# The depthwise convolution of the sample tokens: products with all 31 taps and sums along the taps, in place of 31 small multiply-adds per block

## The chip, the core and the metric

The kernel runs on one core of one Trainium2 chip, in one launch. The metric is the device time of a launch in microseconds (us). A core has five engines with a queue of instructions each, which run beside each other and wait for each other by semaphores: TensorE (PE: matmuls, and PEld for its weight loads), VectorE (DVE), ScalarE (ACT), GpSimd (POOL) and SyncE (SP, here the queue for DMA transfers). Within a queue the order is fixed when the program is built. Matmuls write to PSUM, eight banks of 512 fp32 values per partition; weights and activations lie in SBUF.

## The reference

One step of a two-layer decoder trunk with width 1024, for 272 prompt tokens (16 of them meta tokens) and 8 running sequences of 8 new tokens each. A layer is an FFN half step, a mixer, and a second FFN half step. The mixer projects the normed input to many parts; one branch is gated linear attention, the other a causal depthwise convolution of 31 taps over time, whose inputs for a running sequence start with 30 cached rows:

```python
u = a * jax.nn.sigmoid(ga)
up = jnp.concatenate([conv_buf.astype(u.dtype), u], axis=1)
c = lax.conv_general_dilated(up, w_dw[:, None, :].astype(up.dtype), window_strides=(1,), padding='VALID',
                             dimension_numbers=('NWC', 'WIO', 'NWC'), feature_group_count=CONV_CH) + b_dw
c = jax.nn.silu(rmsnorm(c, conv_norm))
o_conv = c @ w_pw
merged = jax.nn.sigmoid(m_a) * o_gla + jax.nn.sigmoid(m_b) * o_conv
```

All inputs and outputs are fp32.

## The kernel before

Activations lie transposed: 128 channels on the partitions, tokens along the free dimension, eight such blocks (KB) for the 1024 channels. There are 336 tokens in order of prompt, samples and meta (320 in the last layer's later parts). Weights stream from HBM in pieces of up to 128x1024 (`raw`). For fp32 accuracy each piece is split into two parts in a fast matmul format: ACT copies `raw` to `wh` (L214), and VectorE or GpSimd computes `wl = raw - wh` (L215). In the mixer it is GpSimd's work, in the FFNs VectorE's. Each product of a weight block with 336 tokens is three matmuls, eight blocks deep: 24 matmuls.

The mixer of a layer runs in this order: three GLU blocks (`pga`, `pa`), the value projection (`pv`), five more GLU blocks, the query and key projections (`pq`, `pk`), and 24 gate blocks (`pgate`). Into this sequence of products all else is woven. A call of `tick` after every third matmul (L252) takes the next entry of a list of small tasks (the decay chain of the attention, with VectorE's `la`, GpSimd's `lal` and the matmuls `pb`; later the attention heads with `sc`, `probs`, `upd`, `sp`, `pso`, `os`, `upds`, `s`, `o`, `ot`), and then calls `fill` (L231).

`fill` hands out the convolution, as filling for VectorE's queue. It keeps two clocks by a cost table, one of TensorE's work and one of VectorE's (`Clocked`, L98), and as long as VectorE's is less than 1000 ns ahead it takes the next tap from the generator `conv_gen` (L415). A tap is two instructions: a multiply-add of 272 prompt columns (256 in the last layer) into the PSUM bank `acc`, and one of the 64 sample columns into the bank `acs`. Both read `u` (from SBUF) shifted by the tap and the tap's weight, one value per partition, from `vec`, and add to what the tap before left in the bank. The first tap (`TENSOR_SCALAR`) also adds the bias. After tap 31 ACT copies the two banks back over `u` and squares them for the norm (L432 to L436). A task of the last head (`conv_flush`, L752) issues the taps that are left.

PSUM banks come from pools: four for the products (tag `mm`), so that a fifth product has to wait until the first one's bank has been read; two for the small products (`aux`: `upds`, `pso`, `upd`, `nrm`, `pb`); one each for `acc` and `acs` (tags `cv` and `cs`), which the FFNs use as well.

Of the kernel before, what the change touches and what calls it, by code (L numbers as in the profile page):

```python
# [9 lines left out]
F32 = mybir.dt.float32  # L10
F32R = mybir.dt.float32r
U32 = mybir.dt.uint32
AF = mybir.ActivationFunctionType
ALU = mybir.AluOpType

D = 1024
KB = D // 128
DEPTH = 2
META = 16
SEQ = 256  # L20
NS = 8
LS = 8
NSAMP = NS * LS
T = SEQ + NSAMP + META
TY = SEQ + NSAMP
TP = 384
PROMPT = META + SEQ
# [6 lines left out]
TAPS = 31  # L34
# [16 lines left out]
V_F1, V_MIX, V_GLA, V_CN, V_F2, V_BDW = 0, 16, 32, 48, 64, 80  # L51
V_FIN = 96
V_DW = 104
# [44 lines left out]
class Clocked:  # L98
# [4 lines left out]
    def __getattr__(self, name):  # L103
        fn = getattr(self.eng, name)

        def call(*args, **kw):
            out = kw["out"] if "out" in kw else args[0]
            n = 1
            for x in out.shape[1:]:
                n *= x  # L110
            self.add(n * {"reciprocal": 6.25}.get(name, 1.04) + 110.0)
            return fn(*args, **kw)  # L112

        return call
# [3 lines left out]
def trunk_kernel(ctx, tc, wts, x_in, vecs, consts, cumw, masks, wdecay, cache, state,  # L118
                 y_out, sp_out, ss_out, u_out):
    nc = tc.nc  # L120
    PE, ACT, POOL, SP = nc.tensor, nc.scalar, nc.gpsimd, nc.sync
# [5 lines left out]
    DVE = Clocked(nc.vector, dve_time)  # L127
# [10 lines left out]
    tmp = ctx.enter_context(tc.tile_pool(name="tmp", bufs=2))  # L138
# [5 lines left out]
    u = cst.tile([128, KB, UW], F32, name="u")  # L144
    vec = cst.tile([128, NV], F32, name="vec")
# [13 lines left out]
    def vcol(base, l, b, n=KB):  # L159
        return vec[:, base + l * n + b:base + l * n + b + 1]  # L160

    def bank(name, tag="mm", bufs=4):
        return psum.tile([128, 512], F32, tag=tag, name=name, bufs=bufs)
# [202 lines left out]
    def u_sample(b):  # L366
        return u[:, b, UP:UW].rearrange("p (s w) -> p s w", s=NS)

    def mixer(l, norm, next_block):
        last = l == DEPTH - 1  # L370
        n = TY if last else T
        skip = META if last else 0
# [42 lines left out]
        def conv_gen():  # L415
            for b in range(KB):
                while b >= ready[0]:
                    yield 1
                acc = bank("acc", "cv", 1)
                acs = bank("acs", "cs", 1)  # L420
                us = u_sample(b)
                accs = acs[:, 0:NSAMP].rearrange("p (s w) -> p s w", s=NS)
                for i in range(TAPS):
                    wcol = vec[:, V_DW + (l * KB + b) * TAPS + i:V_DW + (l * KB + b) * TAPS + i + 1]
                    for o, src in ((acc[:, skip:PROMPT], u[:, b, skip + i:PROMPT + i]), (accs, us[:, :, i:i + LS])):
                        if i == 0:
                            DVE.tensor_scalar(out=o, in0=src, scalar1=wcol, scalar2=vcol(V_BDW, l, b),
                                              op0=ALU.mult, op1=ALU.add)
                        else:
                            DVE.scalar_tensor_tensor(out=o, in0=src, scalar=wcol, in1=o, op0=ALU.mult, op1=ALU.add)  # L430
                    if i == TAPS - 1:
                        ACT.copy(u[:, b, 0:SEQ], acc[:, META:PROMPT])  # L432
                        ACT.copy(u[:, b, SEQ:TY], acs[:, 0:NSAMP])
                        if not last:
                            ACT.copy(u[:, b, TY:T], acc[:, 0:META])
                        cnorm.add(u[:, b, 0:n], n)  # L436
                    yield 1

        conv = conv_gen()

        def decay_lr():
# [138 lines left out]
        for hd in range(HEADS):  # L580
# [3 lines left out]
                                     op0=ALU.mult, op1=ALU.mult)  # L584
# [240 lines left out]
        w0, w1 = W.use("pw"), W.use("pw")  # L825
# [14 lines left out]
        w0, w1 = W.use("out"), W.use("out")  # L840
# [9 lines left out]
    with tc.manual_schedule():  # L850
# [37 lines left out]
        for l in range(DEPTH):  # L888
            n = TY if l == DEPTH - 1 else T
# [14 lines left out]
        for b in range(KB):  # L904
            DVE.scalar_tensor_tensor(out=h[:, b, 0:TY], in0=h[:, b, 0:TY], scalar=vec[:, V_FIN + b:V_FIN + b + 1],
                                     in1=r[:, 0:TY], op0=ALU.mult, op1=ALU.mult)
# [126 lines left out]
```

## Time and profile before

| | us |
|---|---|
| median of 3 runs | 1631.82 (1631.72 to 1634.56) |
| the profiled execution | 1628.32 |
| its span, from the first instruction to the last | 1626.5 |
| TensorE busy in the span | 1597.0 (98%) |
| VectorE busy in the span | 1079.6 (66%) |
| ACT busy, GpSimd busy | 736.0 (45%), 401.9 (25%) |

The durations below are of the one profiled execution. An instruction's row gives its start and its duration. Instructions of VectorE overlap a little: the next one may start before the end that is shown for the one before it, so what an instruction costs its queue is the time from its start to the next start. Matmuls are pipelined in the same way: those of 336 columns start 0.15 us apart and are shown as 0.32 us long. A row with x2 at its end stands for two instructions in a row and gives the time of both together.

### The profile page before, as it was taken

What the parts mean: (1) busy time and instruction counts of PE and PEld (TensorE: products, weight loads), DVE (VectorE), ACT (ScalarE), POOL (GpSimd) and SP (SyncE); (2) the same over time, 40 slices, a digit from 0 to 9 for tenths busy, and PEclk for the clock granted to TensorE, in tenths of its full rate; (3) what the DMA queues carried; (4) which work ended last, traced back from release to release, by engine and by line L of the source; (5) the groups of instructions that cost most, each with busy time, mean ns of one, the idle gap of its engine ahead of it and who ended that gap; (6) DMA issues with size and microseconds to landing.
All of it is one profiled execution on the core that took longest, in us unless ns stands there. A gap on an engine that the chain in (4) does not pass through costs nothing.

```text
span 1626.5 us, 26968 instructions
## 1 busy us (share of the span) xinstructions
PE 1597.0 (98%) x10516; PEld 1570.4 (97%) x10516; DVE 1079.6 (66%) x2170; ACT 736.0 (45%) x1153; POOL 401.9 (25%) x290
## 2 busy tenths in 40 slices
PE   8999999999999999999999999999999999999997
PEld 7999999999889999999999999999999799999997
DVE  6666445999986666664456564459999766666633
ACT  5433334673546444333343333346645464443432
POOL 0000006576663300000000000066766632000000
PEclk9999999999999999999999999999999999999999
DMA  5554444555544544444446444445555445444352
GB/s 197 189 185 137 136 147 135 163 164 164 157 162 130 165 134 156 142 132 140 145 144 208 150 132 143 153 129 156 174 179 169 156 139 164 148 156 148 120 169 77
DMA packets 77023, 247.78 MB, mean 152 GB/s; under 512 B 8672, under 2 KB 11360, under 8 KB 76640
## 3 DMA queue, kind: packets, MB, share of 16 engines
q1 hardware_dynamic: 76032, 240.16, 46.3%
q10 hardware_dynamic: 864, 5.92, 0.9%
q8 instruction: 82, 1.34, 0.3%
q14 instruction: 45, 0.37, 0.1%
HBM read 230.33 MB, written 15.71 MB: 151 GB/s over the span
## 4 chain that ended last, share of the span: by engine, by line
PE 88%; DVE 6%; DMA 2%; POOL 1%; ACT 1%; issue 1%; SPq 0%; DVEq 0%; POOLq 0%; ACTq 0%
PE pu L134 20%; PE pg L134 20%; PE pd L134 20%; PE pgate L134 9%; PE po L134 4%; PE pw L134 3%; DVE acc L112 2%; PE pa L134 2%; PE pv L134 2%; PE pga L134 2%; PE pk L134 2%; PE pq L134 2%; POOL wl L215 1%; DVE acs L112 1%; PE upds L134 1%
## 5 line engine op out<-in xcount | busy, mean ns | idle before, releaser
L112 DVE TENSOR_TENSOR wl<-raw,wh 128x1024 fp32r<-128x1024 f32 (+3 forms) x331 | 361.7, 1109 | 246.0 <-ACT wh L214 245.4
L214 ACT CAST wh<-raw 128x1024 fp32r<-128x1024 f32 (+4 forms) x457 | 427.3, 954 | 61.1 <-issue 24.9
L215 POOL TENSOR_TENSOR wl<-raw,wh 128x1024 fp32r<-128x1024 f32 (+2 forms) x126 | 283.6, 2270 | 145.2 <-ACT wh L214 135.3
L296 POOL TENSOR_TENSOR ssum<-ssum,sq 128x336 f32<-128x336 f32 (+1 forms) x63 | 56.8, 901 | 1021.9 <-ACT sq L295 1021.7
L112 DVE SCALAR_TENSOR_TENSOR acc<-u,vec,acc 128x272 f32<-128x272 f32 (+1 forms) x480 | 235.1, 490 | 0.0
L134 PE MATMUL pg<-xh,wh 128*128 128x336 f32 (+1 forms) x704 | 223.2, 317 | 6.0 <-ACT wh L214 6.0
L134 PE MATMUL pu<-xh,wh 128*128 128x336 f32 (+1 forms) x704 | 222.1, 315 | 1.4 <-ACT wh L214 1.4
L134 PE MATMUL pu<-xh,wl 128*128 128x336 f32 (+1 forms) x704 | 222.1, 315 | 0.3 <-DVE wl L112 0.3
L134 PE MATMUL pg<-xh,wl 128*128 128x336 f32 (+1 forms) x704 | 222.1, 315 | 0.0
L134 PE MATMUL pg<-xl,wh 128*128 128x336 f32 (+1 forms) x704 | 221.9, 315 | 0.0
L134 PE MATMUL pu<-xl,wh 128*128 128x336 f32 (+1 forms) x704 | 221.9, 315 | 0.0
L134 PE MATMUL pd<-act_hi,wh 128*128 128x336 f32 (+1 forms) x704 | 221.0, 314 | 0.0
L134 PE MATMUL pd<-act_hi,wl 128*128 128x336 f32 (+1 forms) x704 | 220.4, 313 | 0.0
L134 PE MATMUL pd<-act_lo,wh 128*128 128x336 f32 (+1 forms) x704 | 220.2, 313 | 0.0
L134 PEld LDWEIGHTS pg<-xh,wh 128*128 128x128 f32 x704 | 133.0, 189 | 6.4 <-ACT wh L214 6.0
L352 ACT CAST act_hi<-pu 128x336 fp32r<-128x336 f32 (+1 forms) x88 | 38.4, 436 | 218.1 <-DVE pu L112 218.1
L112 DVE SCALAR_TENSOR_TENSOR acs<-u,vec,acs 128x64 f32<-128x64 f32 x480 | 135.3, 282 | 0.0
L134 PEld LDWEIGHTS pu<-xh,wh 128*128 128x128 f32 x704 | 132.9, 189 | 1.8 <-ACT wh L214 1.8
L134 PEld LDWEIGHTS pu<-xh,wl 128*128 128x128 f32 x704 | 132.9, 189 | 0.8 <-DVE wl L112 0.8
L134 PEld LDWEIGHTS pg<-xl,wh 128*128 128x128 f32 x704 | 133.0, 189 | 0.4
L134 PEld LDWEIGHTS pg<-xh,wl 128*128 128x128 f32 x704 | 132.9, 189 | 0.2 <-DVE wl L112 0.2
L134 PEld LDWEIGHTS pu<-xl,wh 128*128 128x128 f32 x704 | 132.9, 189 | 0.0
(209 smaller groups left out, 3229.7 us busy)
## 6 DMA issues: line engine op xcount, KB each, us to landing
raw<-in_wts SPq DMA_DIRECT2D x303, 512.0 KB, 3.6
raw<-in_wts SPq DMA_DIRECT2D x64, 384.0 KB, 3.6
raw<-in_wts SPq DMA_DIRECT2D x64, 320.0 KB, 3.0
s<-in_state SPq DMA_DIRECT2D x16, 512.0 KB, 5.5
out_ss<-s SPq DMA_DIRECT2D x16, 512.0 KB, 5.1
raw<-in_wts SPq DMA_DIRECT2D x16, 344.0 KB, 3.3
u<-in_cache ACTq DMA_DIRECT2D x2, 2424.0 KB, 11.6
out_u<-u SPq DMA_DIRECT2D x16, 303.0 KB, 4.6
```

Source lines behind the costliest of these rows:

```text
L112: return fn(*args, **kw)
L134: PE.matmul(out, a, b, start=start, stop=stop)
L214: ACT.copy(wh[:, cs], raw[:, cs])
L215: eng.tensor_tensor(out=wl[:, cs], in0=raw[:, cs], in1=wh[:, cs].bitcast(F32), op=ALU.subtract)
L296: eng.tensor_tensor(out=self.sum[:, 0:n], in0=self.sum[:, 0:n], in1=sq[:, 0:n], op=ALU.add)
L352: ACT.copy(ah[:, j, 0:n], pu[:, 0:n])
```

## The change

The prompt columns keep their 31 multiply-adds. The sample columns no longer have any. In their place, at four points of a block, two sequences are done at once: one product of `u`'s windows (2 sequences x 8 outputs x 31 taps, read as an overlapping view) with the 31 weights of the block, repeated by a stride of zero, into a PSUM bank (496 of its 512 columns), and two taps of the prompt later one sum along the innermost 31 into 2 x 8 columns of an SBUF tile, `acs`. The bias is added by ACT, whose copy back to `u` becomes an activation with a bias. The planner's clock counts a sum by its input.

```diff
--- before.py
+++ after.py
@@ -108,6 +108,8 @@
             n = 1
             for x in out.shape[1:]:
                 n *= x
+            if name == "tensor_reduce":
+                n *= kw["in_"].shape[-1]
             self.add(n * {"reciprocal": 6.25}.get(name, 1.04) + 110.0)
             return fn(*args, **kw)
 
@@ -417,20 +419,31 @@
                 while b >= ready[0]:
                     yield 1
                 acc = bank("acc", "cv", 1)
-                acs = bank("acs", "cs", 1)
-                us = u_sample(b)
-                accs = acs[:, 0:NSAMP].rearrange("p (s w) -> p s w", s=NS)
+                acs = tmp.tile([128, NS, LS], F32, tag="acs", name="acs", bufs=2)
+                taps = vec[:, V_DW + (l * KB + b) * TAPS:V_DW + (l * KB + b + 1) * TAPS]
                 for i in range(TAPS):
                     wcol = vec[:, V_DW + (l * KB + b) * TAPS + i:V_DW + (l * KB + b) * TAPS + i + 1]
-                    for o, src in ((acc[:, skip:PROMPT], u[:, b, skip + i:PROMPT + i]), (accs, us[:, :, i:i + LS])):
-                        if i == 0:
-                            DVE.tensor_scalar(out=o, in0=src, scalar1=wcol, scalar2=vcol(V_BDW, l, b),
-                                              op0=ALU.mult, op1=ALU.add)
+                    o, src = acc[:, skip:PROMPT], u[:, b, skip + i:PROMPT + i]
+                    if i == 0:
+                        DVE.tensor_scalar(out=o, in0=src, scalar1=wcol, scalar2=vcol(V_BDW, l, b),
+                                          op0=ALU.mult, op1=ALU.add)
+                    else:
+                        DVE.scalar_tensor_tensor(out=o, in0=src, scalar=wcol, in1=o, op0=ALU.mult, op1=ALU.add)
+                    part, step = divmod(i - 3, 6)
+                    if 0 <= part < 4 and step in (0, 2):
+                        ss = slice(2 * part, 2 * part + 2)
+                        if step == 0:
+                            prod = bank("prod", "cs", 1)[:, 0:2 * LS * TAPS].rearrange("p (s w i) -> p s w i", s=2, w=LS)
+                            w0 = u_sample(b)[:, ss, 0:LS]
+                            win = bass.AP(tensor=w0.tensor, offset=w0.offset, ap=list(w0.ap) + [[1, TAPS]])
+                            DVE.tensor_tensor(out=prod, in0=win, op=ALU.mult,
+                                              in1=taps.unsqueeze(1).unsqueeze(1).to_broadcast([128, 2, LS, TAPS]))
                         else:
-                            DVE.scalar_tensor_tensor(out=o, in0=src, scalar=wcol, in1=o, op0=ALU.mult, op1=ALU.add)
+                            DVE.tensor_reduce(out=acs[:, ss], in_=prod, op=ALU.add, axis=mybir.AxisListType.X)
                     if i == TAPS - 1:
                         ACT.copy(u[:, b, 0:SEQ], acc[:, META:PROMPT])
-                        ACT.copy(u[:, b, SEQ:TY], acs[:, 0:NSAMP])
+                        ACT.activation(u[:, b, SEQ:TY], acs.rearrange("p s w -> p (s w)"), AF.Identity,
+                                       bias=vcol(V_BDW, l, b))
                         if not last:
                             ACT.copy(u[:, b, TY:T], acc[:, 0:META])
                         cnorm.add(u[:, b, 0:n], n)
```

Two places of VectorE's queue, as the programs are built (a row per instruction; xN where equal ones follow each other; in brackets the semaphores that it waits on, of which DVE_49 is VectorE's own).

The start of the first channel block of the first layer, before: `u` is the last of the GLU block's writes, then the taps follow in pairs.

```order
L112 TENSOR_TENSOR u<-pa,gate 128x8x8
L112 TENSOR_SCALAR acc<-u,vec 128x272 [waits DVE_49]
L112 TENSOR_SCALAR acs<-u,vec 128x64
L112 SCALAR_TENSOR_TENSOR acc<-u,vec,acc 128x272 [waits DVE_49]
L112 SCALAR_TENSOR_TENSOR acs<-u,vec,acs 128x64 [waits DVE_49]
```

The same place now:

```order
L114 TENSOR_TENSOR u<-pa,gate 128x8x8
L114 TENSOR_SCALAR acc<-u,vec 128x272 [waits DVE_49]
L114 SCALAR_TENSOR_TENSOR acc<-u,vec,acc 128x272 [waits DVE_49] x3
L114 TENSOR_TENSOR prod<-u,vec 128x496
L114 SCALAR_TENSOR_TENSOR acc<-u,vec,acc 128x272 [waits DVE_49] x2
L114 TENSOR_REDUCE acs<-prod 128x16
L114 SCALAR_TENSOR_TENSOR acc<-u,vec,acc 128x272 [waits DVE_49]
L114 TENSOR_TENSOR pga<-pga,rstd 128x336 [waits PE_49]
```

The `acs` between two `acc` are gone; three of four `acc` now stand directly behind another, and each still waits on VectorE's semaphore.

The decay chain of the first layer, between two GLU blocks, before: `la` are its three instructions on VectorE, and 88 taps stand ahead of the first of them.

```order
L112 SCALAR_TENSOR_TENSOR acs<-u,vec,acs 128x64 [waits DVE_49]
L112 SCALAR_TENSOR_TENSOR la<-pz,la 128x512 [waits DMAHW5_49,Activation_49]
L112 TENSOR_TENSOR pa<-pa,rstd 128x336 [waits PE_49]
L112 TENSOR_TENSOR u<-pa,gate 128x16 [waits DVE_49,Activation_49]
L112 TENSOR_TENSOR u<-pa,gate 128x256
L112 SCALAR_TENSOR_TENSOR la<-pz,la 128x512 [waits Pool_49]
```

And now, with 89 taps, 12 products and 12 sums ahead of it:

```order
L114 TENSOR_REDUCE acs<-prod 128x16
L114 SCALAR_TENSOR_TENSOR acc<-u,vec,acc 128x272 [waits DVE_49] x3
L114 SCALAR_TENSOR_TENSOR la<-pz,la 128x512 [waits DMAHW5_49,Activation_49]
L114 TENSOR_TENSOR pa<-pa,rstd 128x336 [waits PE_49]
L114 TENSOR_TENSOR u<-pa,gate 128x16 [waits DVE_49,Activation_49]
L114 TENSOR_TENSOR u<-pa,gate 128x256
L114 SCALAR_TENSOR_TENSOR la<-pz,la 128x512 [waits Pool_49]
```

The instructions that don't belong to the convolution are the same and in the same order; only the number of taps ahead of each has moved by a few. On TensorE, GpSimd and SyncE nothing has moved.

## Rows read from the trace of the kernel before

**Rows 1.** The page: busy us (share) instructions; VectorE's busy tenths in 40 slices.
```profile
PE 1597.0 (98%) x10516; PEld 1570.4 (97%) x10516; DVE 1079.6 (66%) x2170; ACT 736.0 (45%) x1153; POOL 401.9 (25%) x290
...
DVE  6666445999986666664456564459999766666633
```
**Rows 2.** Stretches: length; busy us of PE, PEld, DVE, ACT, POOL; clock, DMA.
```profile
20.00:262.00 242.00, 242.00 (x1582) 242.00 (x1581) 131.75 (x179) 97.03 (x146) 15.25 (x18) 1.00 0.49 158
...
268.00:486.00 218.00, 212.57 (x1404) 203.12 (x1403) 205.18 (x614) 113.22 (x200) 142.01 (x91) 0.98 0.52 161
1080.00:1290.00 210.00, 205.99 (x1398) 196.30 (x1397) 200.50 (x616) 111.36 (x191) 140.42 (x91) 1.00 0.53 167
```
**Rows 3.** Timeline of VectorE among the taps: start us, us, engine, line, operation.
```profile
296.40 0.50 DVE L112 SCALAR_TENSOR_TENSOR acc<-u,vec,acc 128x272 f32<-128x272 f32 x1
296.81 0.28 DVE L112 SCALAR_TENSOR_TENSOR acs<-u,vec,acs 128x64 f32<-128x64 f32 x1
297.00 0.50 DVE L112 SCALAR_TENSOR_TENSOR acc<-u,vec,acc 128x272 f32<-128x272 f32 x1
```
**Rows 4.** Timeline of VectorE at a query block.
```profile
362.81 0.51 DVE L112 SCALAR_TENSOR_TENSOR pq<-pq,rstd 128x336 f32<-128x336 f32 x1
363.36 0.51 DVE L112 TENSOR_TENSOR qt<-pq,qt 128x336 f32<-128x336 f32 x1
363.78 0.50 DVE L112 SCALAR_TENSOR_TENSOR acc<-u,vec,acc 128x272 f32<-128x272 f32 x1
```
**Rows 5.** Timelines of VectorE and GpSimd at two heads' ot.
```profile
432.68 1.05 DVE L112 SCALAR_TENSOR_TENSOR ot<-ot,vec,rstd 128x336 f32<-128x336 f32 x2
...
454.27 3.52 DVE L112 SCALAR_TENSOR_TENSOR ot<-ot,vec,rstd 128x336 f32<-128x336 f32 x2
457.71 0.49 DVE L112 SCALAR_TENSOR_TENSOR acc<-u,vec,acc 128x272 f32<-128x272 f32 x1
...
454.85 2.57 POOL L215 TENSOR_TENSOR wl<-raw,wh 128x1024 fp32r<-128x1024 f32 x1
```
**Rows 6.** Timelines of VectorE, ACT and TensorE at 322 to 325 us.
```profile
322.25 0.51 DVE L112 TENSOR_TENSOR pga<-pga,rstd 128x336 f32<-128x336 f32 x1
...
324.13 0.45 ACT L546 ACTIVATE gate<-pga 128x336 f32<-128x336 f32 x1
...
324.75 0.32 PE L134 MATMUL pa<-xh,wh 128*128 128x336 f32 x1
```
**Rows 7.** Timelines of four engines, 458 to 462 us, and one stretch.
```profile
459.51 0.50 DVE L112 TENSOR_TENSOR pgate<-pgate,rstd 128x336 f32<-128x336 f32 x1
...
460.11 0.45 ACT L612 ACTIVATE gate<-pgate 128x336 f32<-128x336 f32 x1 [5.33 <-DVE pgate L112]
...
461.39 0.38 ACT L693 COPY os<-pso 128x256 f32<-128x256 f32 x1
...
458.42 0.69 PE L134 MATMUL upds<-v,km 32*128 32x256 f32 x2
461.82 1.13 PE L134 MATMUL upds<-v,km 32*128 32x256 f32 x6 [2.70 <-ACT os L693]
...
462.80:465.40 2.60, 2.60 (x10) 2.53 (x10) 2.60 (x8) 0.00 (x0) 1.55 (x3) 0.52 0.13 43
```
**Rows 8.** Lines of VectorE: count | busy us, mean ns | idle before.
```profile
L112 DVE SCALAR_TENSOR_TENSOR acs<-u,vec,acs 128x64 f32<-128x64 f32 x480 | 135.3, 282 | 0.0
...
L112 DVE RECIPROCAL rstd<-sd 128x336 f32<-128x336 f32 x10 | 22.5, 2250 | 21.7 <-ACT sd L311 21.6
```
**Rows 9.** Waits in both conv stretches: total us, times, longest.
```profile
DVE acc L112 <- ACT u L435: 3.5, 6, 1.5
...
DVE acc L112 <- ACT u L432: 2.2, 4, 1.1
```
**Rows 10.** Lines of GpSimd in the stretch 268 to 486 us.
```profile
L215 POOL TENSOR_TENSOR wl<-raw,wh 128x1024 fp32r<-128x1024 f32 x37 | 88.6, 2414 | 31.6 <-ACT wh L214 31.5
L215 POOL TENSOR_TENSOR wl<-raw,wh 128x688 fp32r<-128x688 f32 x8 | 13.3, 1678 | 6.4 <-ACT wh L214 6.4
```

## The prediction

> **What bounds the kernel now.** I read four views in this order. First the page's busy table and slices [rows 1]: TensorE is busy 98% of the span, VectorE 66% as a mean. The mean hides two stages: VectorE stands at 9 tenths in four slices from 285 to 447 us and in four from 1098 to 1260 us, inside the two layers' mixers. Second, the stretches [rows 2]: in an FFN stretch VectorE has 131.75 us of work in 242 us, but in the conv stretch of the first layer 205.18 of 218, and of the second 200.50 of 210. So VectorE sits idle for 12.8 + 9.5 = 22.3 us in these 428 us. There it is a second bound beside TensorE, and whatever it has to do beyond that idle time must lengthen the stretch. GpSimd is busy for 142.01 of 218 us in the same place. Third, the timeline of VectorE [rows 3 to 5], for what one instruction of each kind costs from its start to the start of the next (the listed durations overlap by some 0.09 us, so they aren't the cost). Fourth, two places where TensorE follows VectorE [rows 6, 7]. At 324.75 us the pa group starts in a bank that ACT's sigmoid had let go of 0.17 us earlier (324.13 + 0.45); that sigmoid needs VectorE's pga product of 322.25. At 459.51 VectorE is late with pgate; ACT's gate, then its copy of os, then TensorE's upds follow at 460.11, 461.39 and 461.82, while TensorE has stood since the two upds matmuls of 458.42. [...]
>
> **What is removed.** 31 small instructions (acs) per channel block in 16 blocks, 496: the 480 multiply-adds of the table of lines [rows 8] and 16 first ones. A tap pair takes 0.60 us, 0.41 for acc and 0.19 for acs [rows 3]. The last acs of a block saves nothing, since the next block waits for ACT's copies of acc anyway [rows 9]. That leaves 480 x 0.19 = 91.2 us off VectorE's queue.
>
> **What is added, and runs on VectorE.** Per block four products and four sums along the taps, each over 496 elements: 128 instructions. One with 336 elements and an operand in PSUM costs 0.42 us (qt, 363.36 to 363.78 [rows 4]); acc (272 elements, 0.41) [rows 3] against acs (64, 0.19) gives about 1.04 ns an element, so 160 more make 0.58 us. 128 x 0.58 = 74.2 us. The sum has no row of its kind. It may be shorter than the product by its missing output (0.5 us), or cost several cycles an element: the slowest VectorE row, RECIPROCAL, takes 2.25 us for 336 [rows 8], which would be 3.3 us for 496. I take 0.58, the price of every one-pass row.
>
> **What the small instructions were hiding.** Each tap adds to the bank that the tap before it wrote, and the order shows a wait on VectorE's own semaphore at nearly each. Before, the acs stood between two acc, and the first acc had ended when the next was due. Now taps stand directly behind each other. The price of such a wait is in the timeline. qt, which reads the pq just written, starts 0.55 us after pq; the next instruction, which needs nothing of qt, 0.42 after it [rows 4]. So 0.13 us for each tap directly behind its predecessor. In the order these are 158 in the first layer and 153 in the second (the others have a product, a sum or another stage's work between them): 311 x 0.13 = 40.4 us. The lower bound is nothing, if the wait were free for this form.
> [...]
>
> **What the products collide with.** The old taps read one operand from SBUF and one from PSUM. The product reads both from SBUF. The trace has such instructions beside GpSimd's: the pair of ot at 432.68, with GpSimd at rest, takes 1.05 us; the pair at 454.27 takes 3.52, and VectorE's next instruction can't start before 457.71, right after GpSimd's wl (454.85 + 2.57 = 457.42) has ended [rows 5]. So a VectorE instruction with two SBUF inputs waits for the end of the GpSimd instruction under way. GpSimd is busy 65% of the stretch, mostly with wl of 2.41 us, some of 1.68 [rows 2, 10]; a product that falls at random waits half of one, near 1.1 us, in 65% of cases. The waits themselves stretch the stage and thin GpSimd's share to some 0.55, so I take 0.6 us: 64 x 0.6 = 38.4 us. The bounds are nothing (the products always miss) and 2.1 us each (a whole wl, as the second ot), 134 us. The sums read PSUM alone.
> [...]
>
> **ACT and TensorE.** ACT's copy of acs becomes an activation with the bias, one for one, on an engine that is busy for 113.22 of 218 us [rows 2]: nothing; if it cost 0.2 us more, 16 of them would be 3 us of ACT time, which ACT's free half covers. TensorE's instructions are the same in number and order. The other instructions of VectorE stand in the same order too; the planner only puts the taps a few places earlier (89 taps instead of 88 ahead of the first la), since it counts the new block cheaper.
>
> **The sum.** -91.2 + 74.2 + 40.4 + 38.4 = +61.8 us of VectorE time, in stretches with 22.3 us of idle time. Of the idle time 5.7 us are the waits of a block's first tap for ACT's copies [rows 9], which stay; the rest are mostly round trips over TensorE and ACT, which a late VectorE no longer waits for. So some 16 us are absorbed, and 46 us reach the end, because TensorE has next to nothing in hand: 0.17 us at 324.75. Nothing of this touches the FFN stages. In the profiled execution (1628.32 us, a span of 1626.5 and 1.8 around it) that makes 1674; the median of the runs shown is 1631.82, 3.5 above, so I forecast 1678 us.
>
> **Rivals.**
> *One of the two waits is free* (taps in a row at 0.41 us, or products that miss GpSimd). For it: no row shows exactly these forms. Against: both prices stand in rows of like instructions. The sum is then about +22, less 10 to 16 absorbed: some +10, 1642 us.
> *Both are free, and it gets faster.* VectorE then has 17 us less to do. The place is the late pgate at 459.51: arriving earlier, it takes away most of the wait for os and the slow clock after it, and shortens its like in the second layer. TensorE is busy for 212.57 of 218 and 205.99 of 210 us [rows 2], so 9.4 us of waits are there to be had, of which I give it 8: 1624 us. It decides as soon as the added waits stay below 17 us in all, a fifth of what the rows give.
> *The sums, or the collisions, are far dearer* (a sum at several cycles an element, or a whole GpSimd instruction for each product): 64 x 1.5 more is 96, which with 46 makes 1774 us or above. For it: no row of a sum, and ot's 2.1 us. Against: a product takes its turn once in some 4 us, while wl is 2.4.
> *It is hidden*: no change, since TensorE is at 98%. Against: VectorE has 22.3 us to spare, and the bank at 324.75 had 0.17.
>
> **Chances and range.** Forecast (1655 to 1712) 0.63; one wait free 0.18; faster 0.09; far dearer 0.08; hidden 0.02. The range takes in the forecast's own bounds (idle time all kept or all used: +40 to +62; a collision of 0.3 to 1.2 us: 19 less to 38 more) and the upper part of the case with one wait free: 1640 to 1712. A measurement of this kernel tells 0.2%, 3.3 us, from no change. Faster by more than that: 0.09; within it: 0.04; slower: 0.87.
>
> **What would show it.** In the changed profile two taps in a row stand 0.53 to 0.54 us apart, and 0.41 if I am wrong. A product shows 0.67 us alone, and up to some 3 us where GpSimd is inside a wl; the mean tells the 38.4. The sum shows 0.67 us at any time. VectorE's idle time in the two stretches falls well below 22 us, TensorE's waits grow by some 20 us in each mixer, first at the pa group behind 324.75 and at upds, and the FFN stages keep their length. The forecast fails if the products' mean is at 0.67, or if VectorE still has idle time to spare.

## The result and the profile after

The changed kernel takes 1695.64 us (median of 4 runs, 1693.38 to 1695.93), the kernel before 1631.77 beside it: a ratio of 1.0385, 95% interval 1.037 to 1.0399, or 63.9 us more. The forecast was 1678 us, its range 1640 to 1712. The profiled execution has a span of 1694.1 us.

Its page, busy times and slices, to be held against [rows 1]:

```profile
PE 1623.9 (96%) x10516; PEld 1586.8 (94%) x10516; DVE 1122.0 (66%) x1802; ACT 737.7 (44%) x1153; POOL 411.6 (24%) x290
PE   8999999898989999999999999998989899999997
DVE  6665437999986656565456564469998856666543
```

VectorE's share is 66% again, and as misleading: the slices at 9 tenths are where the time grew. The same stretches as in [rows 2], an FFN and the two conv stretches, each up to the same place of TensorE's work as there (the last taps are done a little earlier, at 515.3 and 1349.9 us; before, at 486.2 and 1290.1, they ended the stretch):

```profile
core 0: us, PE busy (x) PEld busy (x) DVE busy (x) ACT busy (x) POOL busy (x), PEclk, DMA share, GB/s
20.00:262.00 242.00, 242.00 (x1582) 242.00 (x1582) 131.84 (x179) 96.04 (x145) 14.81 (x17) 1.00 0.48 158
268.00:523.00 255.00, 227.85 (x1415) 212.20 (x1413) 230.08 (x435) 116.97 (x207) 149.01 (x94) 0.95 0.44 139
1117.00:1357.50 240.50, 218.41 (x1393) 204.60 (x1392) 220.95 (x435) 114.97 (x197) 149.12 (x94) 0.96 0.46 147
```

The FFN stretch holds the same 1582 matmuls in the same 242 us. The conv stretches last 255 us instead of 218 and 240.5 instead of 210: 67.5 us, the whole difference of the two spans (1694.1 and 1626.5). TensorE is idle for 27.2 and 22.1 us there (5.4 and 4.0 before), 39.8 us more. The other 27.7 us are in its busy time, 227.85 and 218.41 us instead of 212.57 and 205.99 for the same work; TensorE's mean granted clock is 0.95 and 0.96 there instead of 0.98 and 1.00.

VectorE's timeline at the end of a block, which answers to [rows 3]:

```profile
310.36 0.67 DVE L114 TENSOR_REDUCE acs<-prod 128x16 f32<-128x496 f32 x1
310.94 2.12 DVE L114 SCALAR_TENSOR_TENSOR acc<-u,vec,acc 128x272 f32<-128x272 f32 x4
312.97 0.68 DVE L114 TENSOR_TENSOR prod<-u,vec 128x496 f32<-128x496 f32 x1
313.55 1.04 DVE L114 SCALAR_TENSOR_TENSOR acc<-u,vec,acc 128x272 f32<-128x272 f32 x2
314.50 0.67 DVE L114 TENSOR_REDUCE acs<-prod 128x16 f32<-128x496 f32 x1
315.08 3.74 DVE L114 SCALAR_TENSOR_TENSOR acc<-u,vec,acc 128x272 f32<-128x272 f32 x7
319.58 0.56 DVE L114 TENSOR_SCALAR acc<-u,vec 128x272 f32<-128x272 f32 x1 [0.75 <-ACT u L448]
```

Four taps and the product behind them: 312.97 - 310.94 = 2.03 us, three gaps of 0.54 and one of 0.41. A product and a sum that nothing holds up cost 0.58 each (312.97 to 313.55, 310.36 to 310.94). All products and all sums (shortest, median, longest in ns):

```profile
L114 DVE TENSOR_TENSOR prod<-u,vec x64: 674/1050/2642, 271.1 to 1338.0; 128x496 f32<-128x496 f32 x64
L114 DVE TENSOR_REDUCE acs<-prod x64: 659/667/669, 273.3 to 1343.6; 128x16 f32<-128x496 f32 x64
```

The sum takes 0.66 to 0.67 us whatever GpSimd does, the product 0.67 to 2.64. The longest stands beside a GpSimd instruction (VectorE's timeline first, then GpSimd's):

```profile
437.40 2.64 DVE L114 TENSOR_TENSOR prod<-u,vec 128x496 f32<-128x496 f32 x1
```
```profile
437.14 2.37 POOL L217 TENSOR_TENSOR wl<-raw,wh 128x1024 fp32r<-128x1024 f32 x1 [0.36 <-ACT wh L216]
```

It ends 0.53 us after wl (437.14 + 2.37 = 439.51). The others behave alike: of the 64 products 42 started while a GpSimd instruction was under way, and each of them ended 0.53 to 0.55 us after it; the other 22 took 0.67 to 0.68 us. How the lateness reaches TensorE is in two lists of waits of the first conv stretch, TensorE's and ACT's (total, times, longest, us), and in VectorE's own:

```profile
PE pga L136 <- ACT v L526: 5.4, 1, 5.4
PE upd L136 <- ACT kuT L605: 5.2, 1, 5.2
...
PE upds L136 <- ACT os L706: 2.7, 1, 2.7
```
```profile
ACT u L444 <- DVE acc L114: 41.9, 6, 12.5
ACT wg L622 <- DVE pgate L114: 29.2, 7, 7.3
ACT gate L559 <- DVE pga L114: 23.2, 7, 7.5
```
```profile
DVE acc L114 <- ACT u L448: 5.4, 6, 1.6
DVE s L114 <- PE upds L136: 3.8, 3, 3.2
DVE sp L114 <- ACT sp L671: 3.2, 4, 1.5
```

TensorE waits for ACT, ACT for VectorE. The first of them in ACT's timeline, and behind it TensorE's:

```profile
318.86 0.37 ACT L444 COPY u<-acc 128x256 f32<-128x256 f32 x1 [11.66 <-DVE acc L114]
...
319.97 2.92 ACT L216 CAST wh<-raw 128x1024 fp32r<-128x1024 f32 x3
322.80 0.54 ACT L526 ACTIVATE v<-pv,rT 128x344 f32<-128x344 f32 x1
```
```profile
323.39 0.65 PE L136 MATMUL pga<-xh,wh 128*128 128x336 f32 x1 [5.39 <-ACT v L526]
```

ACT stands 11.66 us for a block's last tap. Three wh casts and the eviction of v are queued behind that copy, and TensorE's pga starts at 323.39, 0.05 us after v has ended. In the chain of waits between 300 and 330 us nearly everything is VectorE:

```profile
by line: DVE acc L114 63.5%; DVE prod L114 23.5%; DVE acs L114 9.6%; issue 2.3%; ACT u L444 1.2%; ACT u L445 0.8%; ACT u L448 0.2%
```

### The profile page after: what moved, and what is told of

Its sections match the earlier page's. It is cut to its first block, busy times and chain, and to the rows that moved or that the text cites. A ratio compares the mean times of both kernels' runs of the same rounds, so it can differ in the third digit from the quotient of the medians.

```text
span 1694.1 us, 26607 instructions
## 1 busy us (share of the span) xinstructions
PE 1623.9 (96%) x10516; PEld 1586.8 (94%) x10516; DVE 1122.0 (66%) x1802; ACT 737.7 (44%) x1153; POOL 411.6 (24%) x290
## 3 DMA queue, kind: packets, MB, share of 16 engines
q1 hardware_dynamic: 76032, 240.16, 44.5%
## 4 chain that ended last, share of the span: by engine, by line
PE 67%; DVE 26%; ACT 3%; issue 2%; DMA 2%; SPq 0%; DVEq 0%; POOL 0%; ACTq 0%
PE pd L136 19%; PE pg L136 19%; PE pu L136 19%; DVE acc L114 12%; DVE prod L114 4%; PE po L136 3%; PE pgate L136 3%; PE pw L136 3%; DVE acs L114 2%; ACT wh L216 1%; DVE rstd L114 1%; DVE u L114 1%; DVE pgate L114 1%; PE upds L136 1%; DVE s L114 1%
## 5 line engine op out<-in xcount | busy, mean ns | idle before, releaser
L217 POOL TENSOR_TENSOR wl<-raw,wh 128x1024 fp32r<-128x1024 f32 (+2 forms) x126 | 289.9, 2318 | 172.7 <-ACT wh L216 153.4
L136 PE MATMUL pgate<-xh,wh 128*128 128x336 f32 (+1 forms) x384 | 136.1, 354 | 4.3 <-ACT wg L622 3.3
```

The costliest lines, as they stand in the source:

```text
L136: PE.matmul(out, a, b, start=start, stop=stop)
L217: eng.tensor_tensor(out=wl[:, cs], in0=raw[:, cs], in1=wh[:, cs].bitcast(F32), op=ALU.subtract)
```

## Experiments

Theory: both waits that the prediction names (a tap for its predecessor, a product for GpSimd) are real, VectorE sets the length of the conv stretches, and what it gets longer the kernel gets longer. Against it stood that either wait is something else, that the order in which the planner lays the work is to blame, or that the lateness costs only through one place in ACT's queue. Ratios are to the kernel before, run beside each. The edits are shortened: `...` and words in parentheses stand for code that is left out.

**e1_two_banks**

```diff
-  o, src = acc[:, skip:PROMPT], ...
+  o, src = (acd if i % 2 and i < 26 else acc)[:, skip:PROMPT], ...
-  prod = bank("prod", "cs", 1)...
+  prod = tmp.tile([128, 512], F32, tag="prod", ...)...
   (tap 1, the first into acd, only multiplies)
+  if i == 25:      ACT.copy(acx, acd)
+  if i == TAPS - 1: DVE.tensor_tensor(out=acc, in0=acc, in1=acx, op=ALU.add)
```

> Taps 1, 3, ... 25 of each block add into a second PSUM bank, so that no tap there reads what the one before it wrote; ACT copies that bank out and one add joins it at the end of the block. The products go to SBUF to free the bank. Theory (a tap waits 0.13 us for the end of the tap before it when it reads that tap's sum): taps of the two banks stand 0.41 us apart instead of 0.54, some 240 of them, -31 us; 16 adds cost 16 x 0.54 = 8.6 us more; VectorE gets 22 us shorter and the time, which follows VectorE one for one, goes from 1695.6 to about 1674. Rival (0.54 is what this form costs behind another of its kind, whoever reads what): taps stay 0.54 us apart and the adds make it 1704.

Measured: 1658.0 us, 1.0156 (1.0132 to 1.018), 37.6 us less than the changed kernel. VectorE's timeline:

```profile
299.75 0.49 DVE L114 SCALAR_TENSOR_TENSOR acc<-u,vec,acc 128x272 f32<-128x272 f32 x1
300.16 0.49 DVE L114 SCALAR_TENSOR_TENSOR acd<-u,vec,acd 128x272 f32<-128x272 f32 x1
300.57 0.50 DVE L114 SCALAR_TENSOR_TENSOR acc<-u,vec,acc 128x272 f32<-128x272 f32 x1
...
307.88 2.66 DVE L114 SCALAR_TENSOR_TENSOR acc<-u,vec,acc 128x272 f32<-128x272 f32 x5
310.64 0.45 DVE L114 TENSOR_TENSOR acc<-acc,acx 128x272 f32<-128x272 f32 x1
```

Same instruction, same bytes: 0.41 us apart when they alternate, (310.64 - 307.88) / 5 = 0.55 in the last five, which share a bank. The wait is that of a tap for its predecessor; the rival falls. Of the 15.6 us by which the gain exceeds the 22 expected, 6 are products that met GpSimd less: 67.2 us from start to next start instead of 73.4. That they are written to SBUF now is not the reason: in e9 below they are too, and take 72.7. Whether a tap waits for the sum itself or for any write to the bank, this run doesn't tell apart. The alternating taps too wait on VectorE's semaphore, but need only the tap two places ahead, and stand 0.41 us apart. Needing the tap right ahead costs 0.55 - 0.41 = 0.14 us here.

**e2_short_splits**

```diff
-  eng.tensor_tensor(out=wl[:, cs], ...)
+  for c0, c1 in four quarters of cs (on GpSimd):
+      eng.tensor_tensor(out=wl[:, c0:c1], ...)
```

> The changed kernel, with each of GpSimd's wl subtractions cut into four instructions of a quarter of the columns. Theory (a product waits for the end of the GpSimd instruction under way): the longest wait falls from some 2 us to 0.6, the products' mean from 1.23 us to about 0.85, -24 us, and the time to about 1672. Rival (a product is slowed as long as GpSimd reads SBUF at all, whatever the length of its instructions): the mean stays at 1.2 us or above, and the time at 1695 or above.

Measured: 1672.9 us, 1.0246 (1.0221 to 1.0271). The products:

```profile
L114 DVE TENSOR_TENSOR prod<-u,vec x64: 675/840/5797, 270.5 to 1314.4; 128x496 f32<-128x496 f32 x64
```

Their mean (63.5 us by 64) is 0.99 us instead of 1.23 (0.85 was expected), and the time falls by 22.8, as expected: a product does wait for GpSimd's instructions to end. The longest, expected at 0.6 us of wait, got longer instead, which is taken up below.

**e3_no_samples and e5_no_samples_priced**

```diff
-  (products and sums; ACT adds the bias to what u holds)
```
```diff
   (e5, besides)
+  if i > 1: dve_time(130.0)        # the planner's clock, no instruction
```

> The changed kernel without products and sums: the convolution of the samples is left out, the taps of the prompt stay. VectorE loses 73 us of products and 38 of sums, and gets back some 14 us, because 108 more taps stand directly behind each other: -97 us, 35 us below the kernel before. Theory (VectorE bounds the mixers of the changed kernel, TensorE those of the kernel before, with at most 9.4 us of waits to win): the time stops at TensorE's own, 1620 to 1627. Rival (VectorE still sets the time at this load): 1599. Rival (TensorE's waits have other causes): 1632, as before.

> As e3_no_samples (the convolution of the samples left out), with one number changed in the planner: it counts a tap at 0.52 us, as it takes, instead of 0.39, so that it spreads the taps over the whole mixer as in the kernel before, instead of having them done by 444 us. The instructions are the same. Theory (in e3_no_samples the taps came faster than VectorE can do them, so its queue ran late in the first half of each mixer and stood idle in the second): VectorE's work is 70 us less than in the changed kernel and now evenly laid, TensorE alone is left, 1620 to 1632. Rival (a tap that waits for its own predecessor costs TensorE time in some other way, whatever the order): 1673 again.

Measured: 1673.4 us, 1.0251 (1.023 to 1.0272), which neither the theory nor a rival had, and 1640.2, 1.0041 (1.0025 to 1.0058). The same instructions, 33 us apart by one number of the planner. VectorE's slices of the first and of the second:

```profile
DVE  6665446689746556654456654466896466666643
```
```profile
DVE  6666445878856666655456564458888576666543
```

In the first the taps are laid as if each cost 0.39 us, faster than VectorE does them (0.53); the other work of VectorE in its queue, pga and pgate, comes late behind them, and when the taps of the first layer are done at 445.1 us VectorE is half idle (29.98 us busy of the 61 that follow). So the order can cost as much as the work. What was left at 1640 shows in the second's ACT timeline:

```profile
305.75 0.37 ACT L432 COPY u<-acc 128x256 f32<-128x256 f32 x1 [5.43 <-DVE acc L114]
...
306.86 0.97 ACT L516 ACTIVATE v<-pv,rT 128x344 f32<-128x344 f32 x2
```

ACT stands 5.43 us for a block's last tap, and the evictions of v behind it in its queue hold TensorE for 4.3 us. Hence the 8 us above the 1632 that I expected at most; e12 below takes these stands away.

**e4_padded_before** (the kernel before, with unused work: three instructions of VectorE more in each block, 48 in all, which I reckoned at 0.4 us each, some 20 us, without any wait)

```diff
+  if i in (7, 15, 23):
+      nc.vector.tensor_scalar(out=pad, in0=u[:, b, i:PROMPT + i], scalar1=wcol, op0=ALU.mult)
```

> [...] As my prediction reckoned (VectorE's idle time of 22 us in the two conv stretches takes up some 16): time +4, 1636. Rival (VectorE's idle time is in round trips that move along when it comes late, so it takes up nothing): +20, 1652.

Measured: 1665.9 us, 1.021 (1.0189 to 1.0231): +34. The pads weren't what I took them for. Their row:

```profile
L433 DVE TENSOR_SCALAR pad<-u,vec x48: 344/579/2399, 272.8 to 1322.0; 128x272 f32<-128x272 f32 x48
```

From start to next start they take 38.2 us in all, 0.27 the shortest and 2.32 the longest. So 38 us of added work made 34 us of time: almost nothing is taken up, as the rival says. One thing isn't told apart here: the pads go past the planner's clock, so that the taps are laid as densely as before although VectorE has more to do, and e3 against e5 shows that this can cost time by itself.

**e6_true_prices** (the changed kernel)

```diff
+  if part in range(4) and step == 0: dve_time(520.0)      # a product
+  if the tap stands behind a tap:    dve_time(130.0)
```

> The changed kernel, with the planner's prices set to what the trace shows (a tap behind a tap 0.52 us instead of 0.39, a product 1.15 instead of 0.63). The instructions are the same. Theory (there VectorE simply has more to do than the mixer is long: 57 us more in conv than before, with the last taps already at the place where they must be done): spreading them only leaves some 70 instructions of each layer for that place, and the time stays at 1685 to 1705. Rival (as in e3_no_samples most of the loss is the order): 1670 or less.

Measured: 1708.4 us, 1.0458 (1.0441 to 1.0476), 13 us worse, and a little above the 1685 to 1705 of the theory. The mixer's first part is nearly as fast as before now (from 268 to 445 us TensorE does 1122 matmuls; 1155 before, 963 in the changed kernel), but then 70 conv instructions of the first layer are left in one piece, and TensorE waits for their end (its timeline):

```profile
526.90 1.48 PE L136 MATMUL nrm<-ssum,ones_d 128*128 128x336 f32 x2 [32.46 <-POOL ssum L298]
```

So in the changed kernel, other than in e3_no_samples, true prices don't help: VectorE has too much to do, and spreading it only moves the lateness to the end. An order between the two wasn't tried.

**e7_banks_and_short_splits** (the edits of the first two together)

> e1_two_banks and e2_short_splits together. The two waits are separate by my theory, so the gains add: the first took 37.6 us off, the second 22.8, so 1695.6 - 60 = 1635. Rival (they share a gain, for example a TensorE stall that either removes): 1645 or more.

Measured: 1641.2 us, 1.005 (1.0035 to 1.0064). That lies between the 1635 expected and the rival's 1645. Of 60 us expected 54 came; the two waits are separate but for 6 us.

**e8_gpsimd_products**

```diff
   (e1, besides)
-  part, step = divmod(i - 3, 6)   # product at step 0, sum at step 2
+  part, step = divmod(i, 6)       # product at step 0, sum at step 5
-  DVE.tensor_tensor(out=prod, ...)
+  POOL.tensor_tensor(out=prod, ...)
```

> e1_two_banks with the products on GpSimd instead of VectorE, each five taps ahead of its sum. VectorE loses the 67 us of products that e1_two_banks showed and then has 268 us of convolution, 43 less than the kernel before. Theory: TensorE alone is left in the mixers, 1620 to 1632. Rival (GpSimd, busy for 149 of 255 us there, gets 64 x 1.2 us more; its queue is in order, so that a product stands behind a wl that waits for ACT, and the sum, and VectorE with it, behind the product): 64 x 1 us or more of new waits, 1650 or above.

Measured: 1686.8 us, 1.0331 (1.0316 to 1.0346). The time is in the rival's range. The product's row, and who waited for products:

```profile
L442 POOL TENSOR_TENSOR prod<-u,vec x64: 1158/1181/1235, 271.1 to 1306.8; 128x496 f32<-128x496 f32 x64
...
  DVE acs L114: 51.9, 28
```

A product costs GpSimd 1.18 us, but VectorE stood 51.9 us in front of 28 sums (the rival had 64 or more).

**e9_late_copies**

```diff
-  acc = bank("acc", "cv", 1)
+  acc = bank("acc", ("cv", "cs")[b % 2], 1)       # (prod in SBUF)
+  if i == 8 and done: done.pop()()                # (the block before: ACT's copies, its norm)
```

> The changed kernel, with ACT's copies of a block issued eight taps into the next block instead of right behind its last tap; the accumulators of successive blocks alternate between two PSUM banks, and the products go to SBUF to free the second. VectorE does the same instructions. Theory (VectorE's lateness reaches TensorE through ACT: its queue is in order, its copy of a block stands up to 11.7 us for the last tap, and the wh splits and evictions that TensorE waits for stand behind it): ACT no longer stands there, TensorE's waits behind ACT shrink, VectorE itself is spared its wait at each block's start, and the time falls from 1695.6 to 1665 to 1682. Rival (VectorE's total alone counts, whichever way its lateness passes): only the waits at the blocks' starts go, some 8 us, 1687 or more.

Measured: 1685.5 us, 1.0326 (1.0312 to 1.034): 10 us less, between the theory's 1682 at most and the rival's 1687 at least, and nearer the rival. ACT's waits for a last tap fell from 41.9 to 14.0 us in the first stretch and TensorE still waits there:

```profile
ACT wg L630 <- DVE pgate L114: 32.1, 8, 6.7
ACT gate L567 <- DVE pga L114: 22.6, 7, 7.5
...
ACT u L449 <- DVE acc L114: 14.0, 3, 9.1
```
```profile
PE upd L136 <- ACT kuT L613: 4.5, 1, 4.5
PE pga L136 <- ACT v L534: 4.5, 1, 4.5
PE pa L136 <- ACT gate L567: 2.9, 1, 2.9
```

The copy was a road that VectorE's lateness took, not its cause: closed, others carry it, and the 10 us are about what VectorE's own convolution got shorter by, 9.5.

**e10_banks_splits_late, e11_before_short_splits, e12_nearly_no_conv_wait**

```diff
   (e10: e7, besides)
-  DVE.tensor_tensor(out=acc, in0=acc, in1=acx, ...); ACT.copy(u[:, b, 0:SEQ], acc)
+  DVE.tensor_tensor(out=u[:, b, 0:SEQ], in0=acc, in1=acx, ...)
+  if i == 8 and done: done.pop()()
   (e11: the kernel before, with the edit of e2)
   (e12: e5, with the edits of e2 and e9)
```

> e7_banks_and_short_splits, with the join of the two banks written straight into u by VectorE (so ACT copies no accumulator out and no block's first tap waits for ACT), and ACT's other work on a block issued eight taps into the next one. VectorE's convolution gets some 6 us shorter than the 324 us there. Theory (as for e9): 1641 falls to 1625 to 1635, at the kernel before or just below it. Rival (what is left of the loss is VectorE's total against TensorE): 1636 to 1641.

> The kernel before with GpSimd's wl subtractions in quarters, and nothing else. Its taps don't collide; only ot, ku and the like do, some 10 us of VectorE in all. Theory (VectorE just keeps up in the kernel before, so a few us less change little; TensorE's own waits there are 13 us in both mixers): 1626 to 1632. Rival (GpSimd's 378 further instructions make wl late): above 1635.

> e5_no_samples_priced (the convolution of the samples left out, taps counted at 0.52 us) with late copies from alternating banks as in e9_late_copies and GpSimd's splits in quarters as in e2_short_splits. It asks what any better convolution could win here. Theory (what was left in e5_no_samples_priced were two stands of TensorE of 4.3 us, in which ACT waited 5.4 us for a block's last tap with the eviction of v behind it): these go, and the time is TensorE's alone, 1620 to 1628, 0.5% below the kernel before at most. Rival (the 1640 has another cause, such as the order of the rest): 1635 to 1640.

Measured: e10 1639.1 us, 1.0039 (1.0025 to 1.0053), the rival's figure; e11 1629.7, 0.9985 (0.9973 to 0.9997), and e12 1627.2, 0.9966 (0.9955 to 0.9978), both as the theory had it. The last is what TensorE needs when VectorE's convolution is no longer in its way: 5 us less than the kernel before. So a lighter convolution could hardly have won more than 0.3% in this place, as far as e12's own order tells, and part of that comes with the short splits alone, as e11 shows. The best complete kernel is the old one with short splits, and its gain is at the edge of what can be told.

**All together.** VectorE's conv instructions (acc, acd, acs, prod, join, pad), each from its start to the start of VectorE's next instruction, added up over the trace (what the next one waits for is in it too):

| kernel | VectorE's convolution, us | more than before | time, us | more than before (1631.8) |
|---|---|---|---|---|
| before | 311.4 | | 1631.8 | |
| e10 | 319.3 | 7.9 | 1639.1 | 7.3 |
| e7 | 324.2 | 12.8 | 1641.2 | 9.4 |
| e1 | 335.2 | 23.8 | 1658.0 | 26.2 |
| e2 | 350.6 | 39.2 | 1672.9 | 41.1 |
| e4 | 350.6 | 39.2 | 1665.9 | 34.1 |
| e9 | 359.3 | 47.9 | 1685.5 | 53.7 |
| after | 368.8 | 57.4 | 1695.6 | 63.8 |
| e12 | 278.0 | -33.4 | 1627.2 | -4.6 |
| e5 | 282.5 | -28.9 | 1640.2 | 8.4 |
| e3 | 284.5 | -26.9 | 1673.4 | 41.6 |
| e11 | 311.5 | 0.1 | 1629.7 | -2.1 |
| e8 | 321.4 | 10.0 | 1686.8 | 55.0 |
| e6 | 382.2 | 70.8 | 1708.4 | 76.6 |

(The medians of before beside these runs lie between 1631.8 and 1633.1.) In the rows down to "after" each added microsecond of VectorE's convolution costs 0.7 to 1.1 us of time, down to the 7.9 us of e10, the least that was tried. It holds for these orders of the work only. With less convolution than before (e12, e5, e3) nothing like it comes back, and the order then counts for more than the sum. In e8 the sum is only 10 us longer, 51.9 us of waits for GpSimd's products included; what made 55 us of that wasn't followed further.

## Why the prediction was right, and where not

**The terms of VectorE's sum held.** Each from start to next start, over the whole trace:

| term | predicted | measured |
|---|---|---|
| 480 small instructions gone | -91.2 | 480 x 0.192 = -92.2 |
| 128 products and sums | +74.2 | 128 x 0.584 = +74.8 |
| taps behind taps | +40.4 | 295 x (0.528 - 0.405) + 16 x (0.587 - 0.461) = +38.3 |
| products beside GpSimd | +38.4 | 73.4 - 64 x 0.584 = +36.0 |
| sum | +61.8 | +56.9 |

Both disputed prices, taken from two-instruction rows of other kinds ([rows 4] and [rows 5]), proved to be within 7% for forms the trace didn't show. e1 and e2 show that they are what I took them for, but for the one long wait in e2 that is told at the end. That a sum doesn't collide with GpSimd was assumed; no row of the kernel before shows a sum. The 64 sums bear it out: 35 started while a GpSimd instruction was under way and 29 did not, and both kinds took 0.659 to 0.669 us. The FFN stages cost nothing, as said. ACT's activation takes 0.35 us where the copy took 0.22, 16 x 0.13 = 2 us of ACT in all; what that made of the time wasn't tried apart.

**The step that failed is the absorption.** I let VectorE's 22.3 us of idle time swallow 16 of the 62 us, and so said +46. The runs show that it swallows next to nothing: 57.4 us became 63.8, e10's 7.9 us 7.3, and where the most was taken up it was 5 us of 39 (e4). The idle time was round trips over ACT and TensorE, and I said that a late VectorE no longer waits for them. It does. As I read them, they are answers to things VectorE itself delivers, and so move back with it: in the first stretch the waits for sp are 3.2 us before and after, those for upds 3.8 us (2.4 before), those of a block's first tap 5.4 (3.5). The idle time by [rows 2], which I wanted to see fall well below 22 us, is 24.9 + 19.6 = 44.5, of which 36.9 lie ahead of the last taps. 11.7 of these are a new kind, short gaps like the 0.03 us between a tap's shown end and the next tap's start (0.8 us before). The longer gaps are 25.2 us there and were 21.5 before: none of that idle time was used up. Where the 6 us beyond 57.4 come from stays open; TensorE's busy time grew by 27.7 us at the lower clock (0.95 and 0.96 instead of 0.98 and 1.00), and no run tells how much of that reached the end. Without the 16 us of absorption the forecast would have been 1694, within 2 us of the result. That would have been luck in part: the terms of the sum were 5 us too dear together, which about makes up for these 6.

**Where TensorE waits** was half right. The size is: its idle time grew by 21.7 and 18.1 us, forecast as some 20 in each mixer. pa and upds are on the list, but the longest stands are pga behind ACT's v and upd behind ACT's kuT, which I hadn't traced; ACT's queue stood up to 12.5 us for a block's last tap. That it doesn't matter which road the lateness takes was shown by e9, not foreseen.

**The planner's earlier taps** I costed at nothing. For this kernel no run speaks against that (e6: true prices make it worse), for a lighter convolution it would have been wrong by 33 us (e3 against e5). What I overlooked is that ACT's and GpSimd's share of a block moves with its last tap: in ACT's queue the copies of the first layer's blocks 4 to 8 stand one to six instructions earlier than before, and GpSimd's `ssum` of these blocks moved too, though I wrote that nothing had moved there.

**The rivals.** One wait free: refuted by e1 and e2. Both free and faster: its pool of 9.4 us of TensorE waits was not far off, for e12, with less conv work in the way, gains 5. Far dearer: the products' longest is 2.64 us, but the mean excess is 0.56, near the 0.6 I took; they came once in 7.7 us of the two stretches (495.5 by 64), not once in 4 as I wrote. Hidden: no.

## What to carry to other kernels

A small instruction between two dependent ones may be doing its work in a wait that comes to light when it goes (here a tap behind a tap took 0.528 us of the queue, a tap ahead of a small instruction 0.405); price the queue that is left, start to start, and not the instructions that leave. Where a planner fills an in-order queue up to the pace of the bounding engine, count every added microsecond there nearly in full (here 0.7 to 1.1), because idle time made of round trips moves along (here VectorE's longer gaps ahead of the last taps were 21.5 us before and 25.2 after). And let the planner's prices be what the trace shows: with work to spare, one wrong price cost 33 us here.

## What was unexpected of the hardware

In e2 one product took 5.80 us although no GpSimd instruction there is longer than 1.31 us. VectorE's row, and GpSimd's beside it:

```profile
343.93 5.80 DVE L114 TENSOR_TENSOR prod<-u,vec 128x496 f32<-128x496 f32 x1
```
```profile
341.46 2.83 POOL L219 TENSOR_TENSOR wl<-raw,wh 128x256 fp32r<-128x256 f32 x4
344.24 1.31 POOL L489 TENSOR_TENSOR lal<-la,lah 128x512 fp32r<-128x512 f32 x1
345.49 0.92 POOL L300 TENSOR_TENSOR ssum<-ssum,sq 128x336 f32<-128x336 f32 x1
346.38 2.81 POOL L219 TENSOR_TENSOR wl<-raw,wh 128x256 fp32r<-128x256 f32 x4
```

GpSimd works from 341.46 to 349.19 without a gap, and the product ends at 349.73, 0.54 us later. So what ended the wait was the end of a row of GpSimd instructions, not that of the one under way. Other products did get in between (the median is 0.84); what decides it stays open.

The pads of e4 read one array from SBUF and write SBUF, and they met GpSimd all the same, 0.34 us at best and 2.40 at worst. The worst in VectorE's timeline, and GpSimd's beside it:

```profile
1182.71 2.40 DVE L433 TENSOR_SCALAR pad<-u,vec 128x272 f32<-128x272 f32 x1
```
```profile
1182.55 2.40 POOL L215 TENSOR_TENSOR wl<-raw,wh 128x1024 fp32r<-128x1024 f32 x1 [2.88 <-ACT wh L214]
```

It ends 0.16 us after wl (1185.11 and 1184.95). I had reckoned the pads as free of any wait for GpSimd, and that was wrong: their median is 0.58 us, where the shortest took 0.34. Why they meet it was not shown; the taps don't (0.47 to 0.50 us for all 480 after the first of each block in the kernel before, 328 of which started while a GpSimd instruction was under way).
